# Squares of the new residual summed on TensorE, tile by tile, in the bank of the factors by token

## The chip, the cores and the metric

The kernel runs on one core of a Trainium2 chip. The metric is the device time in microseconds (us) of one execution, as the median of several runs. The engines are called TensorE (PE in the rows, with its weight loads as PEld), VectorE (DVE), ScalarE (ACT), GpSimd (POOL) and SyncE (SP, which issues most transfers). A float32 product is made of three matmuls of rounded parts: a value is split into H (rounded) and L (what is left), and H·H, L·H and H·L are summed.

## The reference

Two model blocks of two layers each run one behind the other on 512 latent tokens of width 1024; the second has 256 context tokens beside them. Each layer has a mixer and a feed-forward part. The change is in the second block, whose residual goes through a norm both behind and ahead of each part:

```
h = h + gt_m * rms_norm(y, g_post_mix[i])
f = swiglu(modulate(rms_norm(h, g_pre_ffn[i]), sh_f, sc_f), w_ffn_gate[i], w_ffn_up[i], w_ffn_down[i])
h = h + gt_f * rms_norm(f, g_post_ffn[i])
if not last:
    ... the same for the context hc
```

with `rms_norm(x, g) = x * rsqrt(mean(x * x) + eps) * g` over the 1024 features of a token, and `modulate(h, shift, scale) = h * (1 + scale) + shift`.

## The kernel before

Activations lie with features on the 128 partitions and tokens along the row: a matrix of 1024 features is KD = 8 tiles. Tokens are worked on in parts of 256: PA and PB (the latents' halves) and CT (the context). A projection takes weights unit by unit (128 output features); each unit is loaded to `raw`, split into `wH` on ScalarE and `wL` on VectorE (`hl`, L398 and L399), and multiplied by `mm3` (L416) with 24 matmuls for eight input tiles and one part.

`chain2` (L1663 and on) returns what runs between a projection out of a part and the next block's input. Its function `after(sl)` is called for one part of tokens when that part's projection is done. It is a generator: its steps are put beside the projections that follow (`defer`, `advance`), and a scheduler then orders the instructions of each engine by priority and by its own estimate of times; in a built program each engine's order is fixed. A call does this:

- It sums the squares of the projection over features: 128 columns of `acc` at a time are the stationary operand and a column of ones moves, so a 128 x 1 result has one sum per token (L527, `ss`). Square root (L529) and reciprocal (L530) make the factors by token, and `on_features` (L547, `rb`) spreads them over all partitions in a PSUM bank.
- For each of eight feature tiles it multiplies the projection by gain and factors (L1683, `ct`), and adds that to the residual (L1684, `x` or `hc`).
- Where another block follows (`nxt`), `add_square` takes the Square of the new residual on ScalarE (L518, `cs`) and adds it on VectorE to `acc` (L519). Then `rsqrt_steps` sums over features again (`ss`), makes new factors (`rb`), and `modulated` (L563 to L565) makes the next block's input, H on ScalarE and L on VectorE, which the next projection's matmuls read.

The calls with `nxt` are eight: named e2 (behind the even mixer; CT, PA, PB; next input `f2u0`), f20 (behind the first feed-forward part; CT, PA, PB; next input `ou`), and o2 (behind the odd mixer; PA, PB; next input `f2u1`). The two calls f21 at the end have no `nxt` and write the output. L1772 is the evacuation of the feed-forward part's last projections (`f`), L1753 that of its first.

Of the kernel before, what the change touches and what calls it, by code (L numbers as in the profile page):

```python
# [8 lines left out]
F32 = mybir.dt.float32  # L9
F32R = mybir.dt.float32r  # L10
BF = mybir.dt.bfloat16
AF = mybir.ActivationFunctionType
# [4 lines left out]
D = 1024  # L17
KD = 8
# [220 lines left out]
def build(tc, A, out, cst_at, vec_at, chk_at, tap=None, upto=99, mark=lambda n: None):  # L239
    nc = tc.nc  # L240
    V, S, T, G = nc.vector, nc.scalar, nc.tensor, nc.gpsimd
# [11 lines left out]
    def load(dst, src):  # L253
        nc.sync.dma_start(dst, src)
# [5 lines left out]
    def wd(sl):  # L260
        return sl.stop - sl.start
# [5 lines left out]
    state = {}  # L267
# [27 lines left out]
    def bank(tag, cols, name):  # L295
        p, rings = state["pm"]
        return p.tile([128, cols], F32, name=name, tag=tag, bufs=rings[tag], padded_shape=[128, max(cols, 512)])
# [4 lines left out]
    def ax(cols=512, name="ax"):  # L302
        return bank("ax", cols, name)
# [7 lines left out]
    def scr(tag, cols=512):  # L311

        p, w = state["sp"] if tag in ("nt", "sq") else (state["np"], {tag: 256})
        return p.tile([128, w[tag]], F32, name=tag, tag=tag, bufs=2 if tag in ("sq", "cs") else 3)[:, :cols]
# [4 lines left out]
    def C(name):  # L319
        o, n = cst_at[name]  # L320
        return cst[:, o:o + n]

    def vcol(name):
        o, n = vec_at[name]
        return vec[:, o:o + n]

    ident, ones, eps = C("ident"), C("ones"), C("eps")
# [182 lines left out]
    def add_square(acc, v, tag="sq"):  # L510

        w = v.shape[-1]
        if not acc:
            acc.append(state["np"].tile([128, 256], F32, name="acc", tag="acc", bufs=3)[:, :w])
            S.activation(acc[0], v, AF.Square)
        else:
            sq = scr(tag, w)
            S.activation(sq, v, AF.Square)  # L518
            V.tensor_tensor(acc[0], acc[0], sq, OP.add)  # L519

    def rsqrt_cols(sqs, ns, n, off, ring="ax", p=None):

        blocks = [sq[:, c:c + 128] for sq in sqs for c in range(0, sq.shape[-1], 128)]
        pc = bank(ring, 512, "ss")
        sel = ones[:, :1] if ns == 1 else C("half2")
        for b, sq in enumerate(blocks):
            T.matmul(pc[:, ns * b:ns * b + ns], sq, sel, start=True, stop=True)  # L527
        rs = (p or state["np"]).tile([128, 24], F32, name="rstd", tag="rstd", bufs=3)[:, :ns * len(blocks)]
        S.activation(rs, pc[:, :ns * len(blocks)], AF.Sqrt, bias=off, scale=1.0 / n)  # L529
        V.reciprocal(rs, rs)  # L530
        return rs

    def rsqrt_steps(sq, n, out):

        rs = rsqrt_cols([sq], 1, n, eps)
        yield
        out.extend(on_features(rs, 1, [sq.shape[-1]]))

    def on_features(rs, ns, ws, ring="ax"):

        r = 128 // ns
        c, pbs = 0, []
        for w in ws:
            pb = bank(ring, w, "rb")
            for b in range(0, w, 128):
                for i in range(ns):
                    T.matmul(pb[r * i:r * i + r, b:b + 128], rs[:, c:c + 1].to_broadcast([128, r]), ident, start=True, stop=True)  # L547
                    c += 1
            pbs.append(pb)
        return pbs  # L550

    def rsqrt_bcs(sqs, ns, n, ring="ax", p=None):
        return on_features(rsqrt_cols(sqs, ns, n, eps, ring, p), ns, [sq.shape[-1] for sq in sqs], ring)
# [4 lines left out]
    def modulated(xk, rs, a, b, h, sl, ks=range(KD)):  # L558

        for k in ks:  # L560
            t = scr("ct", wd(sl))
            hH, hL = h(0, k, sl), h(1, k, sl)
            V.scalar_tensor_tensor(t, xk(k), a[:, k:k + 1], rs, OP.mult, OP.mult)  # L563
            S.activation(hH, t, AF.Identity, bias=b[:, k:k + 1], scale=1.0)
            V.scalar_tensor_tensor(hL, t, b[:, k:k + 1], hH.bitcast(F32), OP.add, OP.subtract)  # L565
# [33 lines left out]
    def gain(name, g, sc):  # L599
        a = cp.tile([128, KD], F32, name=name)  # L600
        V.scalar_tensor_tensor(a, sc, 1.0, g, OP.add, OP.mult)
        return a

    def sub(m, i):
        return m[:, 8 * i:8 * i + 8]
# [425 lines left out]
    def chain(name, g, sc, sh):  # L1031

        box = {}
        acc = {}

        def after(sl):
            if "h" not in box:
                box["h"] = new_h(name)
                box["a"] = gain(name + "A", g, sc)
            rs = []  # L1040
            yield from rsqrt_steps(acc[sl.start][0], D, rs)
            for k in range(0, KD, 2):
                modulated(lambda k: x[:, k, sl], rs[0], box["a"], sh, box["h"], sl, range(k, k + 2))
                yield
        return box, acc, after

    mark("rglru")
    bf0, acc, after = chain("f0", vcol("nf0"), sub(mod[0], 4), sub(mod[0], 3))
# [6 lines left out]
    bm1, acc, after = chain("m1", vcol("nm1"), sub(mod[1], 1), sub(mod[1], 0))  # L1055
# [3 lines left out]
    bf1, acc, after = chain("f1", vcol("nf1"), sub(mod[1], 4), sub(mod[1], 3))  # L1059
# [5 lines left out]
    be, acc, after = chain("e", vcol("gpm0"), sub(m2[0], 1), sub(m2[0], 0))  # L1065
# [593 lines left out]
    def stream(l, sl):  # L1659
        if sl.start >= SEQ:  # L1660
            return state["hc"], slice(sl.start - SEQ, sl.stop - SEQ), mc2[l]
        return state["x"], sl, m2[l]

    def chain2(l, name, gpost, gate, nxt, yv):

        acc, gains = {}, {}

        def after(sl):
            res, rsl, m = stream(l, sl)
            c = sl.start >= SEQ  # L1670
            if c not in gains:
                a = cp.tile([128, KD], F32, name=f"{name}P{int(c)}")
                V.tensor_tensor(a, vcol(gpost), sub(m, gate), OP.mult)
                n = None
                if nxt:
                    n = gain(f"{name}A{int(c)}", vcol(nxt[1]), sub((mc2 if c else m2)[nxt[0]], nxt[2]))
                gains[c] = a, n
            a, n = gains[c]
            rs, nacc = [], []
            yield from rsqrt_steps(acc[sl.start][0], D, rs)  # L1680
            for k in range(KD):
                t = scr("ct", wd(sl))
                V.scalar_tensor_tensor(t, yv(k, sl), a[:, k:k + 1], rs[0], OP.mult, OP.mult)  # L1683
                V.tensor_tensor(res[:, k, rsl], res[:, k, rsl], t, OP.add)  # L1684
                if nxt:
                    add_square(nacc, res[:, k, rsl], "cs")
                if k % 2:
                    if not nxt:
                        load(out[:, k - 1:k + 1, sl], res[:, k - 1:k + 1, rsl])
                    yield k == KD - 1  # L1690
            if nxt:
                yield from rsqrt_steps(nacc[0], D, rs)
                h = nxt[4]()
                for k in range(0, KD, 2):
                    modulated(lambda k: res[:, k, rsl], rs[1], n, sub((mc2 if c else m2)[nxt[0]], nxt[3]), h, sl, range(k, k + 2))
                    yield
        return acc, after
# [190 lines left out]
    acc, after = chain2(0, "e2", "gom0", 2, (0, "gpf0", 4, 3, hf0), yv)  # L1888
# [6 lines left out]
    fs, cs = [], []  # L1895
    acc, after = chain2(0, "f20", "gof0", 5, (1, "gpm1", 1, 0, ho), lambda n, sl: fs[0][:, n, sl])
# [265 lines left out]
    def yv(n, sl):  # L2162
        return f[:, n, sl]

    acc, after = chain2(1, "o2", "gom1", 2, (1, "gpf1", 4, 3, hf1), yv)
# [4 lines left out]
    acc, after = chain2(1, "f21", "gof1", 5, None, yv)  # L2170
# [21 lines left out]
```

## Time and profile before

| What | Value |
|---|---|
| Time, median of 3 runs | 3222.17 us (3218.04 to 3224.64) |
| The profiled execution's own time | 3225.02 us |
| Its span, first to last instruction | 3223.3 us |
| Mean granted TensorE clock | 0.977 of full speed |
| Shares of the span in the chain of work that ended last | TensorE 61%, issue 9%, VectorE 5%, ScalarE 4% |

All times of rows are of the profiled execution, in us from the start of its span. Busy time is the time in which an engine had an instruction in work; a matmul's duration overlaps the next one's start, so the distance between starts tells what a matmul takes in a stream. The granted clock is a share of full speed (2.4 GHz; half of it is 1.2 GHz).

### The profile page before, as it was taken

The page shows a single profiled execution, that of the slowest core. Times are in us where ns is not written, and L with a number is a line of the kernel's source. Part 1 is how long each engine was busy: PE and PEld are TensorE (multiplying, and loading weights), DVE is VectorE, ACT ScalarE, POOL GpSimd, SP SyncE. Part 2 cuts the span into 40 slices and gives each one's busy share as a digit, 9 for nine tenths or more (in the row PEclk, how much of TensorE's full clock was granted, in tenths as well). Part 3 has the DMA queues.
Part 4 walks back from the last instruction along what each step waited for, and adds up shares of the span by engine and source line. Part 5 has one row for each costly group of instructions (what it writes and reads, how often), then busy time and mean ns, then how long its engine had stood idle before and what let it go on. Part 6 is the DMA issues. An engine that isn't in the chain of part 4 may idle for free.

```text
span 3223.3 us, 51513 instructions
## 1 busy us (share of the span) xinstructions
PE 3072.6 (95%) x20678; PEld 2610.6 (81%) x20678; DVE 2066.8 (64%) x4044; ACT 1472.0 (46%) x2558; POOL 17.4 (1%) x47
## 2 busy tenths in 40 slices
PE   6999999998999999998899999999997989999998
PEld 5788888975888889886667898888987867898887
DVE  7976555788787777668866684443637447572335
ACT  4965333446553335546554562212425436562222
POOL 0000000000000000000100000000000000000000
PEclk9999999997999999999899999999998999999999
DMA  7546654320256554442322433441423221242223
GB/s 233 190 151 219 196 189 163 125 66 7 73 191 202 189 196 164 135 140 90 115 70 92 136 104 118 162 146 62 158 100 131 79 91 47 75 152 94 95 99 101
DMA packets 140927, 414.72 MB, mean 129 GB/s; under 512 B 14224, under 2 KB 37520, under 8 KB 140048
## 3 DMA queue, kind: packets, MB, share of 16 engines
q1 hardware_dynamic: 138656, 400.43, 37.5%
q0 software_dynamic: 2032, 11.01, 1.1%
q8 instruction: 162, 2.65, 0.3%
q14 instruction: 77, 0.63, 0.1%
HBM read 386.74 MB, written 24.64 MB: 128 GB/s over the span
## 4 chain that ended last, share of the span: by engine, by line
PE 61%; issue 9%; DVE 5%; ACT 4%; DMA 1%; POOL 0%; DVEq 0%; ACTq 0%; POOLq 0%
PE mm L416 48%; PE po L1359 2%; PE rb L547 2%; PE ptr L1348 2%; PE S L830 1%; PE S L1402 1%; PE ss L527 1%; ACT DT L1546 1%; ACT wH L398 1%; DVE wL L399 1%; PE po L969 1%; PE sa L1575 1%; PE ptr L975 1%; DVE acc L519 0%; DVE ct L1683 0%
## 5 line engine op out<-in xcount | busy, mean ns | idle before, releaser
L398 ACT CAST wH<-raw 128x1024 fp32r<-128x1024 f32 (+4 forms) x469 | 473.0, 1012 | 1118.5 <-PE mm L416 773.6
L399 DVE TENSOR_TENSOR wL<-raw,wH 128x1024 fp32r<-128x1024 f32 (+4 forms) x469 | 549.7, 1175 | 377.8 <-ACT wH L398 370.4
L416 PE MATMUL mm<-mH,wH 128*128 128x512 f32 (+1 forms) x1104 | 377.7, 349 | 8.5 <-DVE f L1772 5.8
L416 PE MATMUL mm<-mH,wL 128*128 128x512 f32 (+1 forms) x1104 | 374.9, 347 | 1.6 <-DVE wL L399 1.6
L416 PE MATMUL mm<-mL,wH 128*128 128x512 f32 (+1 forms) x1104 | 375.3, 347 | 0.7 <-DVE mL L399 0.7
L589 DVE SCALAR_TENSOR_TENSOR raw<-raw,cond_c 128x1024 f32<-128x1024 f32 x128 | 156.4, 1224 | 154.6 <-DMA raw<-in_ada 154.4
L416 PEld LDWEIGHTS mm<-mH,wH 128*128 128x128 f32 x1104 | 206.0, 189 | 39.6 <-ACT wH L398 6.1
L416 PEld LDWEIGHTS mm<-mH,wL 128*128 128x128 f32 x1104 | 205.0, 189 | 30.5 <-DVE wL L399 2.0
L416 PEld LDWEIGHTS mm<-mL,wH 128*128 128x128 f32 x1104 | 205.5, 189 | 29.3 <-DVE mL L399 0.9
L416 PE MATMUL mm<-f2u0L,wH 128*128 128x512 f32 (+1 forms) x752 | 206.0, 327 | 0.0
L416 PE MATMUL mm<-f2u0H,wH 128*128 128x512 f32 (+1 forms) x752 | 205.7, 326 | 0.0
L416 PE MATMUL mm<-f2u0H,wL 128*128 128x512 f32 (+1 forms) x752 | 205.1, 326 | 0.0
L416 PE MATMUL mm<-f2u1H,wL 128*128 128x512 f32 (+1 forms) x432 | 151.5, 352 | 1.2 <-DVE wL L399 1.1
L416 PE MATMUL mm<-f2u1H,wH 128*128 128x512 f32 (+1 forms) x432 | 150.8, 352 | 0.6 <-ACT nt L1750 0.5
L416 PE MATMUL mm<-f2u1L,wH 128*128 128x512 f32 (+1 forms) x432 | 151.0, 351 | 0.1
L416 PEld LDWEIGHTS mm<-f2u0H,wL 128*128 128x128 f32 x752 | 125.1, 189 | 13.0
L416 PEld LDWEIGHTS mm<-f2u0H,wH 128*128 128x128 f32 x752 | 124.8, 189 | 12.6
L416 PEld LDWEIGHTS mm<-f2u0L,wH 128*128 128x128 f32 x752 | 124.8, 189 | 12.3
L626 DVE SCALAR_TENSOR_TENSOR x<-mm,mod,x 128x256 f32<-128x256 f32 (+1 forms) x112 | 66.0, 596 | 88.6 <-PE mm L416 88.5
L1753 DVE TENSOR_TENSOR nt<-nt,mm 128x512 f32<-128x512 f32 (+1 forms) x52 | 31.4, 605 | 127.3 <-PE mm L416 126.9
L416 PE MATMUL mm<-f0L,wH 128*128 128x512 f32 (+1 forms) x296 | 106.9, 361 | 0.2 <-DVE f0L L565 0.2
L416 PE MATMUL mm<-f0H,wH 128*128 128x512 f32 (+1 forms) x296 | 106.8, 361 | 0.0
(703 smaller groups left out, 7479.9 us busy)
## 6 DMA issues: line engine op xcount, KB each, us to landing
raw<-in_ada SPq DMA_DIRECT2D x192, 512.0 KB, 3.6
raw<-in_fw SPq DMA_DIRECT2D x142, 512.0 KB, 4.1
raw<-in_gw SPq DMA_DIRECT2D x125, 512.0 KB, 3.2
raw<-in_gw SPq DMA_DIRECT2D x45, 384.0 KB, 3.0
raw<-in_owin SPq DMA_DIRECT2D x25, 512.0 KB, 3.2
raw<-in_ewin SPq DMA_DIRECT2D x22, 512.0 KB, 3.3
raw<-in_awin SPq DMA_DIRECT2D x20, 512.0 KB, 3.8
raw<-in_ewout SPq DMA_DIRECT2D x18, 512.0 KB, 3.9
```

Of the source, the lines that this page charges most:

```text
L398: S.copy(H, src)
L399: V.tensor_tensor(L, src, H.bitcast(F32), OP.subtract)
L416: T.matmul(ps, W[w][:, k], h(p, k0 + k, sl), start=first and k == 0 and j == 0, stop=last and k == kt - 1 and j == 2)
L527: T.matmul(pc[:, ns * b:ns * b + ns], sq, sel, start=True, stop=True)
L547: T.matmul(pb[r * i:r * i + r, b:b + 128], rs[:, c:c + 1].to_broadcast([128, r]), ident, start=True, stop=True)
L589: V.scalar_tensor_tensor(junk, r, 1.0, c, OP.mult, OP.mult, accum_out=o[:, j:j + 1])
L626: V.scalar_tensor_tensor(x[:, n, sl], ps, gate[:, n:n + 1], x[:, n, sl], OP.mult, OP.add)
L830: T.matmul(ps, q, k[:, sl], start=j == 0, stop=j == 1)
L969: T.matmul(po[64 * half:64 * half + 64], vw[:, kt, :64], PT, start=kt == 0, stop=kt == b)
L975: T.transpose(pt[:, 128 * i:128 * i + 128], Ps[half][i][:, 128 * kt:128 * kt + 128], ident)
L1348: T.transpose(pt[:kn, c:c + 128], Ps[half][i][:, k0:k0 + kn], ident)
L1359: T.matmul(po[64 * half:64 * half + 64], vs[half], PT[:kn, half * w:half * w + w], start=j == 0, stop=j == len(keys) - 1)
```

## The change

The Square of each new residual tile no longer goes into `acc` on VectorE. It becomes the stationary operand of two matmuls (one for each 128 tokens) which sum over features and accumulate over the eight tiles in two columns of PSUM. Those columns lie in the tile `rb`, behind the 256 columns of the factors that the multiplies read. The helper `rsqrt_of` then makes the factors from these columns.

```
+    def rsqrt_of(ss, n):
+
+        rs = state["np"].tile([128, 24], F32, name="rstd", tag="rstd", bufs=3)[:, :ss.shape[-1]]
+        S.activation(rs, ss, AF.Sqrt, bias=eps, scale=1.0 / n)
+        V.reciprocal(rs, rs)
+        return rs
...
-            rs, nacc = [], []
-            yield from rsqrt_steps(acc[sl.start][0], D, rs)
+            rs = [rsqrt_cols(acc[sl.start], 1, D, eps)]
+            yield
+
+            pb = ax(512, "rb")
+            rb, ss = pb[:, :wd(sl)], pb[:, wd(sl):wd(sl) + wd(sl) // 128]
+            for b in range(0, wd(sl), 128):
+                T.matmul(rb[:, b:b + 128], rs[0][:, b // 128:b // 128 + 1].to_broadcast([128, 128]), ident, start=True, stop=True)
+            rs[0] = rb
             for k in range(KD):
                 t = scr("ct", wd(sl))
                 V.scalar_tensor_tensor(t, yv(k, sl), a[:, k:k + 1], rs[0], OP.mult, OP.mult)
                 V.tensor_tensor(res[:, k, rsl], res[:, k, rsl], t, OP.add)
                 if nxt:
-                    add_square(nacc, res[:, k, rsl], "cs")
+                    sq = scr("cs", wd(sl))
+                    S.activation(sq, res[:, k, rsl], AF.Square)
+                    for b in range(0, wd(sl), 128):
+                        T.matmul(ss[:, b // 128:b // 128 + 1], sq[:, b:b + 128], ones[:, :1], start=k == b == 0, stop=k == KD - 1 and b > 0)
...
             if nxt:
-                yield from rsqrt_steps(nacc[0], D, rs)
+                rn = rsqrt_of(ss, D)
+                yield
+                rs.extend(on_features(rn, 1, [wd(sl)]))
```

In the order of the changed program the multiply is L1696, the add L1697, the Square L1700, the pair of summing matmuls L1702 (`rb<-cst,cs 128x1 x2`, by the tile's name `rb`), the first factors L1692, the second ones L554. A note such as PE_49 names the semaphore, by its engine, that an instruction waits for.

VectorE's order at the end of f20, for PB. Before, from the first multiply by the factors on:

```order
L1683 SCALAR_TENSOR_TENSOR ct<-f_18452,f20P_23214,rb 128x256 [waits PE_49]
L1683 SCALAR_TENSOR_TENSOR ct<-f_18452,f20P_23214,rb 128x256
L399 TENSOR_TENSOR wL<-raw,wH 128x1024 [waits DMAHW5_49,Activation_49]
L1684 TENSOR_TENSOR x_17167<-x_17167,ct 128x256 [waits DVE_49] x2
L1683 SCALAR_TENSOR_TENSOR ct<-f_18452,f20P_23214,rb 128x256
L1683 SCALAR_TENSOR_TENSOR ct<-f_18452,f20P_23214,rb 128x256 [waits DVE_49]
L1684 TENSOR_TENSOR x_17167<-x_17167,ct 128x256 [waits DVE_49]
L399 TENSOR_TENSOR wL<-raw,wH 128x1024 [waits DMAHW6_49,PE_49,Activation_49]
L519 TENSOR_TENSOR acc<-acc,cs 128x256 [waits Activation_49]
L1684 TENSOR_TENSOR x_17167<-x_17167,ct 128x256 [waits DVE_49]
L519 TENSOR_TENSOR acc<-acc,cs 128x256 [waits DVE_49,Activation_49]
L1683 SCALAR_TENSOR_TENSOR ct<-f_18452,f20P_23214,rb 128x256 x2
```
After, from the same multiply on:

```order
L1696 SCALAR_TENSOR_TENSOR ct<-f_18473,f20P_23238,rb 128x256 [waits DVE_49]
L572 SCALAR_TENSOR_TENSOR ouL<-ct,m_98,ouH 128x256 [waits Activation_49] x2
L1697 TENSOR_TENSOR x_17167<-x_17167,ct 128x256 [waits DVE_49]
L1696 SCALAR_TENSOR_TENSOR ct<-f_18473,f20P_23238,rb 128x256 [waits DVE_49,PE_49]
L1697 TENSOR_TENSOR x_17167<-x_17167,ct 128x256 [waits DVE_49]
L1696 SCALAR_TENSOR_TENSOR ct<-f_18473,f20P_23238,rb 128x256 [waits PE_49]
L1697 TENSOR_TENSOR x_17167<-x_17167,ct 128x256 [waits DVE_49]
L1696 SCALAR_TENSOR_TENSOR ct<-f_18473,f20P_23238,rb 128x256 [waits PE_49]
L1697 TENSOR_TENSOR x_17167<-x_17167,ct 128x256 [waits DVE_49]
L1696 SCALAR_TENSOR_TENSOR ct<-f_18473,f20P_23238,rb 128x256 [waits PE_49]
L1697 TENSOR_TENSOR x_17167<-x_17167,ct 128x256 [waits DVE_49]
L1696 SCALAR_TENSOR_TENSOR ct<-f_18473,f20P_23238,rb 128x256 [waits PE_49]
```
The adds to `acc` are gone, and multiplies and adds alternate; each multiply but the first waits for TensorE.

TensorE's order at the same place, before, around the second sums (`ss`) and factors (`rb`) of PB, in the next block's first projection (`ou`):

```order
L416 MATMUL mm<-ouH,wL 128x256
L416 MATMUL mm<-ouH,wH 128x256
L416 MATMUL mm<-ouL,wH 128x256
L416 MATMUL mm<-ouH,wL 128x256
L527 MATMUL ss<-cst,acc 128x1 x2
L416 MATMUL mm<-ouH,wH 128x256
L416 MATMUL mm<-ouL,wH 128x256
L416 MATMUL mm<-ouH,wL 128x256
L416 MATMUL mm<-ouH,wH 128x256
L547 MATMUL rb<-cst,rstd 128x128 x2
L416 MATMUL mm<-ouL,wH 128x256
L416 MATMUL mm<-ouH,wL 128x256
```
After, from some matmuls ahead of the pairs on:

```order
L416 MATMUL mm<-ouH,wH 128x256
L416 MATMUL mm<-ouL,wH 128x256
L416 MATMUL mm<-ouH,wL 128x256
L1702 MATMUL rb<-cst,cs 128x1 x14
L416 MATMUL mm<-ouH,wH 128x256
L1702 MATMUL rb<-cst,cs 128x1 x2
L416 MATMUL mm<-ouL,wH 128x256
L416 MATMUL mm<-ouH,wL 128x256
L416 MATMUL mm<-ouH,wH 128x256
L416 MATMUL mm<-ouL,wH 128x256
```
Seven of the eight pairs stand in one row, with no matmul of the projection between them, and one matmul is ahead of the eighth.

TensorE's order at o2, PA. Before, the second factors, and the matmuls up to those that read the next block's input (`f2u1`):

```order
L547 MATMUL rb<-cst,rstd 128x128 x2
L416 MATMUL mm<-nqH,wL 128x256
L416 MATMUL mm<-gq,wH 128x256 x2
L416 MATMUL mm<-gq,wL 128x256
L416 MATMUL mm<-gq,wH 128x256 x2
L416 MATMUL mm<-gq,wL 128x256
L416 MATMUL mm<-gq,wH 128x256 x2
L416 MATMUL mm<-gq,wL 128x256
L416 MATMUL mm<-gq,wH 128x256 x2
L416 MATMUL mm<-gq,wL 128x256
L416 MATMUL mm<-f2u1H,wH 128x256 x2
L416 MATMUL mm<-f2u1L,wH 128x256
```
After, from some matmuls ahead of the last two pairs on:

```order
L416 MATMUL mm<-gq,wL 128x256
L416 MATMUL mm<-gq,wH 128x256 x2
L416 MATMUL mm<-gq,wL 128x256
L416 MATMUL mm<-gq,wH 128x256 x2
L416 MATMUL mm<-gq,wL 128x256
L416 MATMUL mm<-gq,wH 128x256 x2
L416 MATMUL mm<-gq,wL 128x256
L1702 MATMUL rb<-cst,cs 128x1 x4
L554 MATMUL rb<-cst,rstd 128x128 x2
L527 MATMUL ss<-cst,acc 128x1 x2
L416 MATMUL mm<-f2u1H,wH 128x256 x3
L416 MATMUL mm<-f2u1L,wH 128x256
```
The last two pairs, the second factors and another part's first sums stand directly ahead of the matmuls on `f2u1`; before, other matmuls of the mixer's projection (`nqH`, `gq`) stood between the factors and them.

## Rows read from the trace of the kernel before

**Rows 1.** The page: busy us of each engine (share of the span), instructions.

```profile
PE 3072.6 (95%) x20678; PEld 2610.6 (81%) x20678; DVE 2066.8 (64%) x4044; ACT 1472.0 (46%) x2558; POOL 17.4 (1%) x47
```
**Rows 2.** Busy time by stretch; columns us, PE, PEld, DVE, ACT, POOL, PEclk, DMA.

```profile
1835.00:1860.00 25.00, 24.18 (x220) 23.66 (x219) 22.24 (x46) 14.87 (x34) 0.00 (x0) 1.00 0.37 127
2480.00:2490.00 10.00, 4.82 (x41) 4.62 (x39) 9.96 (x22) 4.92 (x11) 0.00 (x0) 0.94 0.44 159
```
**Rows 3.** PE's waits: total us, times, longest; 1830-1930, 2455-2530, 2805-2865 us.

```profile
PE mm L416 <- DVE wL L399: 2.7, 2, 1.9
...
PE mm L416 <- DVE f L1772: 8.6, 2, 4.7
PE mm L416 <- DVE nkL L399: 6.1, 1, 6.1
...
PE mm L416 <- DVE wL L399: 1.1, 1, 1.1
```
**Rows 4.** Groups by line: ns minimum/median/maximum, first and last start.

```profile
L1683 DVE SCALAR_TENSOR_TENSOR ct<-y,e2P,rb x24: 471/474/479, 1843.8 to 1910.6; 128x256 f32<-128x256 f32 x24
L1683 DVE SCALAR_TENSOR_TENSOR ct<-f,f20P,rb x24: 470/473/483, 2327.3 to 2489.4; 128x256 f32<-128x256 f32 x24
L1683 DVE SCALAR_TENSOR_TENSOR ct<-f,o2P,rb x16: 472/474/480, 2813.9 to 2854.3; 128x256 f32<-128x256 f32 x16
...
L1684 DVE TENSOR_TENSOR x<-x,ct x64: 411/417/422, 1874.3 to 3219.4; 128x256 f32<-128x256 f32 x64
...
L519 DVE TENSOR_TENSOR acc<-acc,cs x63: 409/417/427, 1253.1 to 2858.3; 128x256 f32<-128x256 f32 x63
...
L518 ACT ACTIVATE cs<-x x42: 399/416/465, 1875.2 to 2856.5; 128x256 f32<-128x256 f32 x42
...
L527 PE MATMUL ss<-cst,acc x132: 164/250/353, 223.4 to 3211.8; 128*128 128x1 f32 x132
```
**Rows 5.** PE's timeline at e2: start us, us, instruction (one pair is x4).

```profile
1857.02 0.40 PE L416 MATMUL mm<-o,wH 128*128 128x256 f32 x2
1857.25 0.55 PE L527 MATMUL ss<-cst,acc 128*128 128x1 f32 x4
1857.66 0.36 PE L416 MATMUL mm<-o,wL 128*128 128x256 f32 x1
1857.86 0.40 PE L416 MATMUL mm<-o,wH 128*128 128x256 f32 x2
```
**Rows 6.** The page's costliest groups: busy us, mean ns, idle before.

```profile
L398 ACT CAST wH<-raw 128x1024 fp32r<-128x1024 f32 (+4 forms) x469 | 473.0, 1012 | 1118.5 <-PE mm L416 773.6
L399 DVE TENSOR_TENSOR wL<-raw,wH 128x1024 fp32r<-128x1024 f32 (+4 forms) x469 | 549.7, 1175 | 377.8 <-ACT wH L398 370.4
```
**Rows 7.** PE's timeline at the end of f20, PA and PB.

```profile
2445.20 0.68 PE L547 MATMUL rb<-cst,rstd 128*128 128x128 f32 x4
...
2478.46 0.60 PE L547 MATMUL rb<-cst,rstd 128*128 128x128 f32 x4
...
2490.94 0.58 PE L416 MATMUL mm<-ouH,wH 128*128 128x256 f32 x1 [6.12 <-DVE nkL L399]
...
2491.75 0.93 PE L527 MATMUL ss<-cst,acc 128*128 128x1 f32 x4
2492.54 0.56 PE L416 MATMUL mm<-ouH,wH 128*128 128x256 f32 x1
...
2493.54 1.05 PE L547 MATMUL rb<-cst,rstd 128*128 128x128 f32 x4
```
**Rows 8.** The timeline at the end of the program (f21), all engines.

```profile
3210.89 0.42 DVE L519 TENSOR_TENSOR acc<-acc,sq 128x256 f32<-128x256 f32 x1 [0.54 <-ACT sq L518]
...
3211.46 0.58 PE L527 MATMUL ss<-cst,acc 128*128 128x1 f32 x4 [1.58 <-DVE acc L519]
3212.07 0.26 ACT L529 ACTIVATE rstd<-ss,cst 128x2 f32<-128x2 f32 x1 [1.22 <-PE ss L527]
3212.37 0.17 DVE L530 RECIPROCAL rstd<-rstd 128x2 f32<-128x2 f32 x1 [1.06 <-ACT rstd L529]
```
## The prediction

> **What bounds the kernel now.** I read the page first. TensorE is busy 95% of the span, VectorE 64%, ScalarE less [rows 1], so I ask of every edit what it adds to TensorE's stream and what it makes TensorE wait for. The other views are of the stretches in which the changed function runs with squares: e2 (CT, PA, PB) from 1844 us on, f20 from 2327 (CT) to 2494 (PB's end), o2 from 2814 [rows 4, 7]. Busy time by stretch shows two kinds of place [rows 2]. At e2, CT to PB, TensorE has 24.18 of 25 us and VectorE 22.24: TensorE is the bound, VectorE has little room. At the end of f20 TensorE has 4.82 of 10 us and VectorE 9.96: there VectorE is the bound. TensorE's waits agree [rows 3]: at e2 2.7 us in all, at the end of f20 14.7, at o2 1.1 for weights; everywhere the waited-for engine is VectorE.
>
> **The change, part by part.** What goes: the sum of squares was seven adds a call on VectorE and one pair of one-column matmuls at its end. Of the 63 adds [rows 4] seven stand in an earlier function, so 56 go, in eight calls. They cost VectorE 0.42 us each, some 0.34 us where several follow each other: 56 × 0.34 = 19 us of VectorE. That is worth time only where TensorE waits for VectorE.
>
> What comes: eight pairs a call in place of one, so 56 pairs more on TensorE. The nearest row is the old pair itself, the same shapes. It starts at 1857.25, the next matmul at 1857.66 (0.41 us), the one after 0.20 later instead of 0.12 [rows 5]: **0.47 to 0.49 us a pair** with what it delays. 56 × 0.47 = 26.3 us. At six of the eight sites TensorE is busy or paced by the rounds below: 42 × 0.47 = **+19.7**. Nothing hides it there. At f20 PA and PB it is part of a sum of its own.
>
> What changes shape: the sums now stand in the bank of the factors, which VectorE reads. In the changed order every multiply but the first of a call carries a wait for TensorE, that is for the pair of the tile before. So a call becomes a ring: pair (TensorE), multiply, add (VectorE), Square (ScalarE), pair. Before, VectorE ran two multiplies and two adds ahead and the summing trailed. The engine times are 0.41 + 0.47 + 0.42 + 0.42 = 1.72 [rows 4, 5]; a hand-over between engines takes 0.03 (pair to root), 0.04 (root to reciprocal) or 0.15 us (add to pair) [rows 8], four of them about 0.3. **One round is 2.02 us** if nothing stands between.
>
> Here a rule speaks against the change. The Trainium skill, "PSUM — Partial Sum Buffer", section "PSUM bank collisions raise a hardware error", says that two engines must not touch the same bank and quadrant at once, not even at different columns, and that semaphores should guard by bank. That explains the wait on a tile that VectorE doesn't read; with guards by address alone, the sum would be the 26.3 us of pairs less some relief. No row of before shows it, since none has two such users in a bank; the changed order does.
>
> In front of each pair TensorE has n matmuls of 256 columns at 0.12 us (two start in 0.23, [rows 5]). With n × 0.12 + 0.47 ≥ 2.02, n ≥ 13, the ring hides. Counted in the changed order: e2 CT 22, 20, 19, 13, 13, 13, 13; e2 PB 24, 13, 19, 18, 13, 17, 21; o2 PB 22, 24, 24, 24, 24, 20, 13; f20 CT 7 to 14 matmuls of 512 columns, at 0.23 us. These just hide it, so I give the four of them 1.2 + 0.7 + 0.3 + 0.5 = 2.7 us for rounds a little longer. But e2 PA has 20, 20, 24, 24, 24, **0, 0**, and o2 PA 14, 20, 24, 24, 24, 12, **0**. Each zero exposes 2.02 − 0.47 = 1.55. Behind the last pair stand root (0.26), reciprocal (0.17) and hand-overs, 0.62 in all, then the first multiply and the first ScalarE cast of the next block's input, about 1.0; before, 13 (o2) to 22 (e2) other matmuls covered this, now none does: 1.6. So e2 PA is 2 × 1.55 + 0.5 (the input's other tiles come at VectorE's pace) + 1.6 = 5.2, o2 PA 1.55 + 0.5 + 0.3 + 1.6 = 3.9. Together with the 2.7: **+11.8**. After such holes the clock falls: behind a wait of 6.12 us matmuls stand 0.21 apart and a pair holds TensorE 0.79 us [rows 7]. For two smaller holes I take 1.5 each: **+3** (0 to 6). Of the 3.8 us of waits for weights at e2 and o2 [rows 3] half may go, since VectorE has less to do: **−2** (0 to −4).
>
> f20 PA and PB: from PA's first factors to PB's second ones it was 2493.54 − 2445.20 = 48.3 us, 33.3 for PA and 15.1 for PB [rows 7]. PA afterwards: 184 matmuls × 0.12 = 22.1, eight pairs 3.8, other sums and factors 0.9, and 1.7 left of waits, 28.5; the 8.6 us of waits for the evacuation (f, L1772) mostly go, because VectorE now alternates between the ring and the evacuations. That is −5. PB: its first multiply is now queued behind PA's next-block input: two casts of 1.18 [rows 6] and eleven multiplies of some 0.40, 6.7 us; the first pair comes at 9.0. Then all pairs but the last stand on TensorE in one row with no matmul between. Nothing covers seven rounds, at the lower clock (pair 0.9, round 2.5): 17.5. With the last pair, root, factors and some slow matmuls about 29 against 15.1: +14. The next projection's matmuls, their evacuation (nkL) and weight casts are queued behind. Net **+9** (5 to 13).
>
> The sum: 19.7 + 11.8 + 3 − 2 + 9 = 41.5, rounded to **+41**. The profiled execution took 3225.0 us (span 3223.3), so 3266 by it. It lay 2.9 us above the median of the three runs, so I say **3263**.
>
> **The rivals.** (A) The forecast, chance 0.50, own range +30 to +55, that is 3252 to 3277.
> (B) The ring hides everywhere, or the program has the time for it elsewhere: only the pairs are paid, and relief and f20 cancel. +20 to +28, 3242 to 3250. For it: the six sites mostly have n ≥ 13. Against: the zeros in the order, and f20 PB. Chance 0.20.
> (C) Rounds are longer: a weight cast on ScalarE (1.01 us) or VectorE (1.18) [rows 6] falls into the ring in half of the rounds. At e2 and o2 20 rounds exceed their cover by 0.8: 16 us; at f20 PB seven by 1.05: 7. 41 + 23 = +64, 3286. For it: VectorE's 22.24 of 25 us [rows 2] means that casts must stand somewhere between. Against: the order can place them while the ring waits. Chance 0.17.
> (D) The other side: VectorE's relief is what counts. If the ring hides, the freed 19 us remove TensorE's waits at e2, f20 and o2 (2.7 + 14.7 + 1.1 = 18.5) and behind them some 5 us (an estimate: 60 matmuls at 0.21 instead of 0.12, [rows 7]), while f20's pairs fall into its idle time. 19.7 − 23.5 = −4; it decides from f20 PB's rounds being covered and a pair under 0.40 us, and at 0.33 it gives −10, 3212. For it: 14.7 us of waits at f20 really are for VectorE. Against: the pair's price is read in TensorE's stream, and the seven uncovered rounds are in the order. Chance of faster 0.06.
> (E) The same with half of these gains: 19.7 − 18.5 = +1, no change that can be measured. Chance 0.07.
>
> **How the numbers follow.** About 0.2% (6.4 us) is what a measurement of this kernel can tell from no change. Slower is A, B and C: 0.87; same 0.07; faster 0.06. The time is A's, 3263. The range takes in B's lower part and C's middle, with the bounds of the unknown costs (f20 5 to 13, clock 0 to 6, relief 0 to −4): 3236 to 3294; outside remain D, E and the long end of C, some 0.2.
>
> **What would show it.** In the profile after: 64 pairs under the new line at some 0.25 us a pass, TensorE's busy time up by about 20 us; multiplies on VectorE waiting for TensorE, spaced by 2.0 us or more within a call; at e2 PA and o2 PA new waits of TensorE for Square, around 1.5 us each, and for the next block's input; at f20 PB a stretch of some 17 us in which TensorE does pairs alone, at a lower granted clock, and the waits for f L1772 much shorter. Wrong it would be if pairs cost under 0.3 us in the stream, if the multiplies don't wait, or if PA's evacuation waits stay as they were (then +46 or more).

## The result

| | Median, us | Lowest to highest | Runs |
|---|---|---|---|
| Before | 3220.1 | 3217.4 to 3224.6 | 4 |
| After | 3266.7 | 3264.8 to 3274.3 | 4 |

The change makes the kernel slower: ratio 1.0149, 95% interval 1.0137 to 1.0161, some 48 us of 3220 (44 to 52). The forecast was 3263 with a range of 3236 to 3294. The profiled execution took 3274.3 us (span 3272.2), 7.6 above the median.

The page of the changed kernel, busy times and the shares of the chain, which answer to [rows 1]:

```profile
span 3272.2 us, 51884 instructions
PE 3112.3 (95%) x20902; PEld 2642.9 (81%) x20902; DVE 2055.5 (63%) x3988; ACT 1466.0 (45%) x2554; POOL 17.4 (1%) x47
...
PE 64%; issue 8%; ACT 4%; DVE 4%; DMA 0%; POOL 0%; ACTq 0%; DVEq 0%; POOLq 0%
```
The span is 48.9 us longer, TensorE's busy time 39.7, and VectorE's 11.3 shorter. TensorE's share stays 95%, so the page alone doesn't show the new waits. Busy time also counts pairs and matmuls that the lower clock stretches, which is one reason why it grew by more than the 20 us that the forecast named.

The multiplies by the factors grouped by line (VectorE; ns minimum, median, maximum; first and last start), and below them what VectorE sat idle for ahead of them (us, times):

```profile
L1696 DVE SCALAR_TENSOR_TENSOR ct<-y,e2P,rb x24: 471/480/483, 1847.2 to 1935.3; 128x256 f32<-128x256 f32 x24
L1696 DVE SCALAR_TENSOR_TENSOR ct<-f,f20P,rb x24: 475/480/481, 2349.0 to 2523.6; 128x256 f32<-128x256 f32 x24
L1696 DVE SCALAR_TENSOR_TENSOR ct<-f,o2P,rb x16: 473/476/481, 2848.0 to 2910.2; 128x256 f32<-128x256 f32 x16
L1696 DVE SCALAR_TENSOR_TENSOR ct<-f,f21P,rb x16: 470/473/481, 3242.6 to 3267.6; 128x256 f32<-128x256 f32 x16
...
  PE rb L1702: 32.3, 27
```
Against [rows 4] a multiply takes as long as before, but VectorE waits 32.3 us in 27 places for the pairs. The first starts also divide the span into stages. The row for f21 of the kernel before, which [rows 4] leave out:

```profile
L1683 DVE SCALAR_TENSOR_TENSOR ct<-f,f21P,rb x16: 471/472/480, 3193.1 to 3218.7; 128x256 f32<-128x256 f32 x16
```
From e2 to f20 it was 483.5 us and is 501.8 (+18.3), from f20 to o2 486.6 and 499.0 (+12.4), from o2 to f21 379.2 and 394.6 (+15.4). The 3.4 us ahead of e2's first multiply are not the change's: nothing is edited there, and over this study's profiled executions that multiply came anywhere from 1834.7 to 1847.2. Stages have a spread too: where two kernels do the same calls in the same way, a stage differed by 0.1 to 3.2 us between their executions.

TensorE's waits in three stretches (e2, the end of f20, o2), as in [rows 3]:

```profile
PE rb L1702 <- ACT cs L1700: 3.9, 3, 1.6
PE rb L554 <- DVE rstd L537: 0.9, 1, 0.9
PE mm L416 <- ACT f2u0H L571: 0.7, 1, 0.7
...
PE rb L1702 <- ACT cs L1700: 15.8, 7, 6.5
PE mm L416 <- DVE nkL L399: 1.4, 1, 1.4
...
PE rb L1702 <- ACT cs L1700: 3.2, 2, 1.9
PE mm L416 <- ACT f2u1H L571: 1.9, 2, 1.1
...
PE rb L554 <- DVE rstd L537: 1.4, 2, 0.8
```
The waits for `wL` and for f (L1772) are gone; the forecast had half of the first and most of the second going. In their place TensorE waits for Squares, and at e2 and o2 for second factors and for the next block's input. The Squares at the end of f20 cost 15.8 us in seven places.

Busy time by stretch, columns as in [rows 2]; the last column but two is the granted clock:

```profile
1845.00:1870.00 25.00, 24.98 (x201) 23.86 (x201) 16.27 (x32) 12.54 (x30) 0.00 (x0) 1.00 0.41 142
1895.00:1920.00 25.00, 19.52 (x128) 18.84 (x128) 14.31 (x33) 11.43 (x23) 0.00 (x0) 0.80 0.11 39
2508.00:2518.00 10.00, 3.77 (x16) 3.43 (x16) 3.62 (x8) 1.66 (x4) 0.00 (x0) 0.50 0.00 0
```
At e2 CT TensorE is still full, and VectorE, at 22.24 of 25 in the nearest stretch of [rows 2], has fallen to 16.27: it waits. What the ring costs there is not idle time of TensorE but longer pairs, as shown below. Around e2 PA's end TensorE has 19.52 of 25, and the clock is 0.80. In the middle of f20 PB TensorE has 3.77 of 10 us, VectorE 3.62 and ScalarE 1.66: no engine is busy half of the time, each waits for the next one, and the granted clock is 0.50, its lower level of 1.2 GHz.

One round of the ring at e2 PA, engines together (start, duration, engine, instruction, idle before and whom for):

```profile
1898.17 0.61 PE L1702 MATMUL rb<-cst,cs 128*128 128x1 f32 x4 [0.78 <-ACT cs L1700]
1898.82 0.48 DVE L1696 SCALAR_TENSOR_TENSOR ct<-y,e2P,rb 128x256 f32<-128x256 f32 x1 [1.61 <-PE rb L1702]
1899.33 0.42 DVE L1697 TENSOR_TENSOR x<-x,ct 128x256 f32<-128x256 f32 x1
1899.85 0.42 ACT L1700 ACTIVATE cs<-x 128x256 f32<-128x256 f32 x1 [1.73 <-DVE x L1697]
1900.32 0.61 PE L1702 MATMUL rb<-cst,cs 128*128 128x1 f32 x4 [1.54 <-ACT cs L1700]
...
1902.49 1.01 PE L1702 MATMUL rb<-cst,cs 128*128 128x1 f32 x4 [1.56 <-ACT cs L1700]
...
1904.35 1.19 PE L554 MATMUL rb<-cst,rstd 128*128 128x128 f32 x4 [0.85 <-DVE rstd L537]
...
1906.93 1.01 PE L416 MATMUL mm<-f2u0H,wH 128*128 128x256 f32 x3 [0.75 <-ACT f2u0H L571]
```
Pair, multiply, add, Square, pair: from 1898.17 to 1900.32 is 2.15 us, with 2.17 to the next. The forecast said 2.02. The multiply starts 0.65 us behind the start of the pair, whose four passes take 0.61; the forecast had put in 0.41 for the pair, the distance to the next matmul's start. The hand-overs (0.04, 0.03, 0.10 and 0.05) are shorter than its 0.3. Behind the last pair stand the second factors at 1904.35 and the first matmul on the next input at 1906.93, with only PB's first sums (`ss`) between them.

TensorE's timeline at f20 PB, to be held against [rows 7]:

```profile
2498.38 0.61 PE L1692 MATMUL rb<-cst,rstd 128*128 128x128 f32 x4
...
2507.13 1.02 PE L1702 MATMUL rb<-cst,cs 128*128 128x1 f32 x4 [6.46 <-ACT cs L1700]
2509.68 1.01 PE L1702 MATMUL rb<-cst,cs 128*128 128x1 f32 x4 [1.54 <-ACT cs L1700]
2512.26 1.02 PE L1702 MATMUL rb<-cst,cs 128*128 128x1 f32 x4 [1.56 <-ACT cs L1700]
...
2522.57 1.01 PE L1702 MATMUL rb<-cst,cs 128*128 128x1 f32 x4 [1.56 <-ACT cs L1700]
...
2524.95 0.58 PE L416 MATMUL mm<-ouH,wH 128*128 128x256 f32 x1 [1.37 <-DVE nkL L399]
...
2528.32 1.05 PE L554 MATMUL rb<-cst,rstd 128*128 128x128 f32 x4
```
From PB's first factors to its second ones it is now 29.9 us, against 15.1; forecast 29. The rounds are 2.55 to 2.58 us long (forecast 2.5), and the first pair comes 8.75 us behind the factors (forecast 9.0).

### The profile page after: what moved, and what is told of

Read it like the earlier page. It is cut to its first block, busy times and chain, and to the rows that moved or that the text cites. A ratio compares the mean times of both kernels' runs of the same rounds, so it can differ in the third digit from the quotient of the medians.

```text
span 3272.2 us, 51884 instructions
## 1 busy us (share of the span) xinstructions
PE 3112.3 (95%) x20902; PEld 2642.9 (81%) x20902; DVE 2055.5 (63%) x3988; ACT 1466.0 (45%) x2554; POOL 17.4 (1%) x47
## 4 chain that ended last, share of the span: by engine, by line
PE 64%; issue 8%; ACT 4%; DVE 4%; DMA 0%; POOL 0%; ACTq 0%; DVEq 0%; POOLq 0%
PE mm L416 50%; PE po L1366 2%; PE ptr L1355 2%; PE rb L554 1%; PE S L837 1%; PE rb L1702 1%; PE S L1409 1%; PE ss L527 1%; ACT DT L1553 1%; PE po L976 1%; ACT wH L398 1%; PE sa L1582 1%; PE ptr L982 1%; ACT P L1342 0%; PE st L1627 0%
## 5 line engine op out<-in xcount | busy, mean ns | idle before, releaser
L399 DVE TENSOR_TENSOR wL<-raw,wH 128x1024 fp32r<-128x1024 f32 (+4 forms) x469 | 549.9, 1175 | 370.7 <-ACT wH L398 363.4
L416 PEld LDWEIGHTS mm<-f2u0L,wH 128*128 128x128 f32 x752 | 126.2, 191 | 13.1
```

Of the source, the lines that this page charges most:

```text
L399: V.tensor_tensor(L, src, H.bitcast(F32), OP.subtract)
L416: T.matmul(ps, W[w][:, k], h(p, k0 + k, sl), start=first and k == 0 and j == 0, stop=last and k == kt - 1 and j == 2)
```

## The experiments

All were timed beside the kernel before on the same chip. A ratio is to the kernel before, with its 95% interval; the us behind it are its share of 3220.

**A bank of its own for the sums.**

```
-            rb, ss = pb[:, :wd(sl)], pb[:, wd(sl):wd(sl) + wd(sl) // 128]
+            rb = pb[:, :wd(sl)]
+            ss = ax(512, "ssq")[:, :wd(sl) // 128] if nxt else None
```

> The pairs stay, but their two columns stand in a bank of their own; in the built order no multiply but the first of a call waits for TensorE any more. My theory (pairs cost 0.47 us each in TensorE's stream, and the ring through the shared bank costs about as much again): 56 x 0.47 = 26 us of pairs remain, less up to 10 us for VectorE's relief and for pairs that fall into TensorE's idle time at f20, so +16 to +26 against before, about 3236 to 3246; TensorE's waits for the Square fall from 23 us to under 5. Rival 1 (the pairs themselves cost it all, 46.6 / 56 = 0.83 us each): it stays at about 3265. Rival 2 (VectorE's relief is what counts once the ring is gone): 3220 or less.

Measured: 3238.8 us, ratio 1.0054 (1.0039 to 1.0069), +17 us. Both rivals fall: with the same 64 pairs in the program, nearly two thirds of the loss are gone once the pairs and the factors don't share a bank: 31 us, 24 to 37 by the two intervals. No multiply sat idle for a pair in this kernel, and TensorE's waits for Squares in the three stretches fell from 22.9 us to 3.6, at e2 and at the end of f20:

```profile
PE ssq L1703 <- ACT cs L1701: 0.2, 1, 0.2
...
PE ssq L1703 <- ACT cs L1701: 3.4, 3, 1.5
```
A pair in this kernel, at e2 (PEld is the weight load, here of the Square's columns):

```profile
1853.84 0.40 PE L416 MATMUL mm<-o,wH 128*128 128x256 f32 x2
1853.96 0.53 PEld L1703 LDWEIGHTS ssq<-cst,cs 128*128 128x128 f32 x4
...
1854.08 0.50 PE L1703 MATMUL ssq<-cst,cs 128*128 128x1 f32 x4
...
1854.44 0.36 PE L416 MATMUL mm<-o,wL 128*128 128x256 f32 x1
...
1854.64 0.28 PE L416 MATMUL mm<-o,wH 128*128 128x256 f32 x1
```
The first load starts at 1853.96, under matmuls in flight, and the pair takes TensorE from 1854.08 on; four starts (two matmuls, the pair, one matmul) use 0.80 us, of which three matmuls are 0.36: 0.44 a pair. The changed kernel at the same place of e2 CT:

```profile
1858.79 0.42 ACT L1700 ACTIVATE cs<-hc 128x256 f32<-128x256 f32 x1
...
1859.26 0.52 PEld L1702 LDWEIGHTS rb<-cst,cs 128*128 128x128 f32 x4 [0.19 <-ACT cs L1700]
1859.26 0.61 PE L1702 MATMUL rb<-cst,cs 128*128 128x1 f32 x4
...
1859.73 0.48 PE L416 MATMUL mm<-o,wH 128*128 128x256 f32 x2
```
Here the Square ends at 1859.21 and the load can start only at 1859.26; the next matmul starts 0.47 behind the pair, and the pair itself stood 0.15 later than the stream would have let it. Worked out in this way over the pairs that have matmuls ahead of them and no wait in their own row, a pair takes 0.62 us on average at e2 and o2 in the changed kernel (30 pairs), 0.48 at e2 with a bank of its own (20 pairs). The Trainium skill, "PSUM — Partial Sum Buffer", section "Engine vs sequencer instructions", says that TensorE's queue lets a weight load overlap matmuls in flight; these rows agree for the kernel with a bank of its own, and in the ring the load starts only when the last matmul is nearly done, since its operand is made just in time.

**Pairs beside the adds, into a bank that nobody reads.** To the kernel before:

```
+            more = ax(512, "ssq")[:, :wd(sl) // 128] if nxt else None
...
-                    add_square(nacc, res[:, k, rsl], "cs")
+                    sq = add_square(nacc, res[:, k, rsl], "cs")
+                    for b in range(0, wd(sl), 128):
+                        T.matmul(more[:, b // 128:b // 128 + 1], sq[:, b:b + 128], ones[:, :1], start=k == b == 0, stop=k == KD - 1 and b > 0)
```

`add_square` here also returns the tile that holds the Square.

> The kernel before, with the adds on VectorE and the old sums kept, plus the same pairs of one-column matmuls on each of the eight squares of a call, into a bank of their own that nobody reads: the price of 64 pairs without ring and without relief. My theory: 64 x 0.47 = 30 us, of which the 16 pairs at f20 PA and PB may lie in idle time: +22 to +31, 3242 to 3251. Rival 1 (a pair costs 0.8 us): +50, 3270. Rival 2 (a pair costs only what its four passes take beyond their overlap, some 0.1 us each way): under +15, 3235 or less.

Measured: 3246.8 us, ratio 1.0076 (1.0051 to 1.0102), +24.5 us for 64 pairs, 0.38 a pair (0.26 to 0.51). Both rivals fall, the second one narrowly (+16 is the lower end of the interval, and it had said under +15). By its three stages the profiled execution was 12.0, 8.8 and 6.8 us longer than before's, 27.6 in all, 0.43 a pair.

**The same pairs, in the bank of the factors.** The edit above, with `more` behind the factors as in the change:

```
-            yield from rsqrt_steps(acc[sl.start][0], D, rs)
...
+            pb = ax(512, "rb")
+            rb, more = pb[:, :wd(sl)], pb[:, wd(sl):wd(sl) + wd(sl) // 128]
...
```

> As the run with pairs beside the kept adds, but the pairs' columns, which nobody reads, stand in the bank of the factors: adds, pairs and ring together, without VectorE's relief. My theory (the ring through the shared bank costs about 29 us by itself, the difference between the changed kernel and the one with a bank of its own): 3247 + 29 and some more, since an add on VectorE now stands in the ring: 3272 to 3285. Rival (the 29 us are not the ring, but come from the squares' sum being ready late): within 8 us of the run with pairs beside, 3255 or less.

Measured: 3275.9 us, ratio 1.0174 (1.0157 to 1.0191), +56 us: 31 more than in a bank of their own (22 to 41). Here nobody needs the sums, so they can't be late; only the shared bank is different, and with it the order that the scheduler makes. This is the plainest evidence for the ring. Between the changed kernel and the one with its own bank it was 48 − 17 = 31 as well. The tile `rb` and the bank are the same 512 columns here, so the runs don't tell a wait that goes by tile from one that goes by bank.

**VectorE's relief alone.** To the kernel before:

```
-                    add_square(nacc, res[:, k, rsl], "cs")
+                    if nacc:
+                        S.activation(scr("cs", wd(sl)), res[:, k, rsl], AF.Square)
+                    else:
+                        add_square(nacc, res[:, k, rsl], "cs")
```

> The kernel before without the seven adds of squares in a call (the second sums of a call cover its first feature tile alone; the Squares are still taken, the pair at the end stays): VectorE's relief by itself, 56 x 0.34 = 19 us of VectorE. My theory: TensorE is the bound nearly everywhere, so only f20 PA and PB and some waits for weights give anything: -2 to -9, 3211 to 3218. Rival 1 (relief removes all of the 18.5 us of waits for VectorE): -18 or more, under 3203. Rival 2 (nothing): within 2 us of before.

Measured: 3207.7 us, ratio 0.9960 (0.9947 to 0.9973), −13 us (−17 to −9). That is more than my theory gave and less than the rival's 18. By stages: e2 −1.7, f20 −5.6, o2 −3.4, together −10.7.

**f20 as before.** To the changed kernel:

```
-            rb, ss = pb[:, :wd(sl)], pb[:, wd(sl):wd(sl) + wd(sl) // 128]
+            rb, ss, nacc = pb[:, :wd(sl)], pb[:, wd(sl):wd(sl) + wd(sl) // 128], []
+            pairs = name != "f20"
...
-                if nxt:
+                if nxt and not pairs:
+                    add_square(nacc, res[:, k, rsl], "cs")
+                elif nxt:
...
-                rn = rsqrt_of(ss, D)
+                rn = rsqrt_of(ss, D) if pairs else rsqrt_cols([nacc[0]], 1, D, eps)
```

> The changed kernel with the three calls of f20 done as before (adds on VectorE, one pair at the end); e2 and o2 as in the change. My theory (every call pays for itself, by the distances between the same points of the two traces f20 costs 3.8 at CT and 8.5 to 9.3 at PA and PB): 12 to 13 us less than the changed kernel, 3253 to 3255. Rival (the seven uncovered rounds at f20 PB lie beside waits that would be there anyway): less than 6 us less, 3261 or more.

Measured: 3251.8 us, ratio 1.0100 (1.0076 to 1.0124), +32 us: 16 less than the changed kernel. The rival falls; my 12 to 13 lies within the noise of that difference. The stage from f20 to o2 was 484.4 us in it, 14.6 less than the changed kernel's 499.0, and 2.2 less than in the kernel before, which does f20 in the same way.

**PA of e2 and o2 as before.** The same edit with another condition:

```
+            pairs = not (name in ("e2", "o2") and sl.start == 0)
```

> The changed kernel with e2 PA and o2 PA done as before (the two calls whose last pairs have no matmul ahead of them in TensorE's order); CT and PB of e2, all of f20, and o2 PB as in the change. My theory: seven pairs (3.3 us), the holes (5.2 and 3.9) and the slower clock behind them (1.5) go at each: 16 to 20 us less than the changed kernel, 3247 to 3251. Rival (the holes are a matter of the order and turn up at the next call instead): under 10 us less, above 3257.

Measured: 3237.9 us, ratio 1.0071 (1.0052 to 1.0090), +23 us: 25 less than the changed kernel, where I had said 16 to 20. The stage e2 to f20 is 488.7 us, 13.1 less than in the changed kernel, and o2 to f21 385.9, 8.7 less, together 21.8. Another 3.2 lie at f20, where both kernels do the same, and may be the executions' own spread. The rival's price falls. At e2 TensorE has no wait for a Square left. At o2 the rival's mechanism does show: the last pair of PB now has three matmuls ahead of it, and TensorE waits there for its Square,

```profile
PE rb L1705 <- ACT cs L1703: 1.4, 1, 1.4
```
which it did not do at PB in the changed kernel. The two calls with pairs that have no matmul ahead of them bear nearly half of the loss, their own pairs included.

**Two tiles at a time, in the shared bank.** In the changed kernel the pairs of tiles k − 1 and k are issued behind every odd k:

```
-                    for b in range(0, wd(sl), 128):
-                        T.matmul(ss[:, b // 128:b // 128 + 1], sq[:, b:b + 128], ones[:, :1], start=k == b == 0, stop=k == KD - 1 and b > 0)
+                    two = [sqs, sq] if k % 2 else []
+                    sqs = sq
+                    for i, v in enumerate(two):
+                        for b in range(0, wd(sl), 128):
+                            T.matmul(ss[:, b // 128:b // 128 + 1], v[:, b:b + 128], ones[:, :1], start=k == 1 and i == b == 0, stop=k == KD - 1 and i == 1 and b > 0)
```

> The changed kernel, same shared bank and the same 64 pairs, but the pairs of two tiles are issued together behind every second tile: VectorE waits for TensorE once in two tiles. My theory: a round of two tiles takes two multiplies, two adds, one Square and two pairs, some 3.2 us in place of 4.0, and the matmuls ahead of it cover nearly all of that at e2 and o2; most of the ring's 29 us goes: 3240 to 3250. Rival (what counts is that a pair and a reader are in one bank, however rarely they wait): above 3258.

Measured: 3236.8 us, ratio 1.0051 (1.0034 to 1.0068), +16 us, as good as a bank of its own and 3 us below the 3240 of my theory. What VectorE sat idle for ahead of the multiplies in this kernel:

```profile
  PE rb L1705: 17.1, 22
```
It still waits 22 times for pairs, but 17.1 us in all, and one of two multiplies runs ahead of the wait. TensorE has no wait for a Square left at e2 and o2. The rival falls: sharing a bank does not cost by itself; a hand-over in every tile does, with the order that the scheduler builds around it.

**Pairs at f20 PA and PB alone, in a bank of their own.** The edits of the own bank and of the condition together, to the changed kernel; with them e2, o2 and f20 CT are as in the kernel before (`c` is true for CT):

```
+            rb, nacc = pb[:, :wd(sl)], []
+            pairs = name == "f20" and not c
+            ss = ax(512, "ssq")[:, :wd(sl) // 128] if nxt and pairs else None
...
```

> The kernel before, with pairs in a bank of their own at f20 PA and PB alone, where TensorE waits for VectorE: 14 adds less on VectorE, 14 more pairs that may fall into TensorE's idle time. By the run with a bank of its own everywhere (that stage was 5.9 us longer, of which CT's seven pairs are about 3): -2 to +4, 3217 to 3223. Rival (the pairs are free there and the relief of 5.6 us in this stage, seen without the adds, stays): -4 to -6, 3213 to 3215.

Measured: 3223.0 us, ratio 1.0013 (1.0003 to 1.0023), +4 us (1 to 7), at the upper end of my theory; the rival falls. At the end of f20 TensorE waits for f (L1772 of before) once, 3.9 us, instead of twice, 8.6, and not for `nkL`, but 3.4 us for Squares. So 7.4 us less of waits stand against 14 more pairs, some 5 us at 0.38, and yet the stage from f20 to o2 is 488.2 us against 486.6. Where the rest went is not shown.

**The adds on GpSimd.** To the kernel before, for the squares of these calls:

```
-    def add_square(acc, v, tag="sq"):
+    def add_square(acc, v, tag="sq", E=None):
...
-            V.tensor_tensor(acc[0], acc[0], sq, OP.add)
+            (E or V).tensor_tensor(acc[0], acc[0], sq, OP.add)
...
-                    add_square(nacc, res[:, k, rsl], "cs")
+                    add_square(nacc, res[:, k, rsl], "cs", G)
```

> The kernel before with the adds of a call's squares on GpSimd instead of VectorE, nothing on TensorE: VectorE's relief, which was worth 11 to 13 us when the adds were left out, without the pairs' price. My theory: -4 to -12, 3207 to 3215, if seven GpSimd adds keep pace with the tiles. Rival (an add takes GpSimd above 1.3 us, or slows VectorE beside it, so the second sums come late): at or above 3222.

Measured: 3245.2 us, ratio 1.0074 (1.0058 to 1.0090), +24 us; the rival held. The adds on GpSimd (ns minimum, median, maximum), and a wait of TensorE at e2:

```profile
L519 POOL TENSOR_TENSOR acc<-acc,cs x56: 722/788/3959, 1849.6 to 2879.8; 128x256 f32<-128x256 f32 x56
```
```profile
PE ss L527 <- POOL acc L519: 11.4, 3, 5.3
```
The median add takes 0.79 us, but the longest 3.96, and all 56 take 63.5 us; the second sums wait for the last of them, 21.6 us over e2, f20 and o2. The trace shows where the long ones lie. The twelve adds with VectorE idle beside them took 0.72 to 0.73 us. All eleven above 1.4 us ran beside a weight split on VectorE (L399) for 0.8 us or more; the longest, at 1885.60, beside two, 2.4 us of them, and 1.4 us of VectorE's other work. VectorE's own adds stayed at 0.42.

**Half of the adds on GpSimd.** To the kernel before (the first tile's Square makes `nacc`; `nacc2` is a second `acc`):

```
+                    if k < 4:
+                        ...
+                            G.tensor_tensor(nacc[0], nacc[0], sq, OP.add)
+                    else:
+                        add_square(nacc2, res[:, k, rsl], "cs")
...
-                yield from rsqrt_steps(nacc[0], D, rs)
+                V.tensor_tensor(nacc2[0], nacc2[0], nacc[0], OP.add)
+                yield from rsqrt_steps(nacc2[0], D, rs)
```

> The kernel before, with the squares of a call's first four tiles summed on GpSimd and of the last four on VectorE, and one more add on VectorE to join them: four adds a call on VectorE in place of seven, nothing more on TensorE. My theory: GpSimd's three adds (1.1 us each on average in the run with all seven there) end before VectorE's last ones, so the chain's end is no later, and three sevenths of the 11 to 13 us of relief come: -3 to -6, 3214 to 3217. Rival (GpSimd beside VectorE takes several us for an add, so the joining add waits): 3222 or more.

Measured: 3217.4 us, ratio 1.0000 (0.9991 to 1.0009). Neither the gain of the theory nor the rival's loss: a gain above 3 us is excluded. By its stages the profiled execution was 4.6 us shorter, of which the timed runs show nothing, so this stays inconclusive. No version that keeps the sums whole beats the kernel before.

## Why the prediction was right, point by point

**What bounds the kernel.** Right. TensorE's work and waits made the time, and VectorE's relief moved little: 13 us when nothing takes its place, 4 to 5 us where pairs come in (pairs beside against own bank: 24.5 − 17 = 7 us, of which eight more pairs are 3; in the shared bank 56 − 48 = 8).

**The parts of the sum.** Of the 48 us, 56 pairs at 0.38 are 21 and the ring 31; the −4 that is left over goes to the relief. The sum was grouped by places, and there it says:

| Place | Forecast, us | Measured by stage, us |
|---|---|---|
| e2: pairs 9.9, rounds and holes 7.1, clock 1.5, relief −1.4 | 17.1 | 18.3 |
| f20: CT 3.8, PA and PB 9 | 12.8 | 12.4 |
| o2: pairs 6.6, rounds and holes 4.2, clock 1.5, relief −0.5 | 11.8 | 15.4 |

At f20 both halves were right: PA 27.7 us from its first factors (2470.69) to PB's (forecast 28.5), PB 29.9 (29). At e2 PA the five waits in the rows above sum to 5.5 us, where 5.2 was forecast. That e2 as a whole fits within 1.2 us is in part luck: by the run with PA as before, PA cost 13.1 (forecast 10.0), so CT and PB together cost 5.2 (forecast 7.1).

**What was mis-sized.** First, "One round is 2.02 us". The bare ring takes 2.15, because VectorE waits for all of the pair's 0.61 and not for its 0.41. So 13 matmuls ahead don't quite hide it: the four rounds of e2 CT with 13 ahead are 2.15 us long, the ring's own time.

Second, the term "42 × 0.47". In the 37 covered rounds of e2, o2 and f20 CT a pair takes 0.61 beyond the matmuls, since its Square comes just when TensorE gets there. That is 0.14 × 37 = 5 us, of which the 2.7 us for rounds a little longer stood for half. Rounds with 19 to 24 matmuls ahead, which the bare ring would fit into, pay it too: ScalarE often has something else ahead of the Square. In 22 of the 64 tiles that is a weight cast, at o2 in 11 of 16. At e2 PA, where the add was done at 1893.74:

```profile
1893.83 1.05 ACT L398 CAST wH<-raw 128x1024 fp32r<-128x1024 f32 x1 [1.55 <-PE mm L416]
1894.78 0.41 ACT L1700 ACTIVATE cs<-x 128x256 f32<-128x256 f32 x1
```
Elsewhere it is the evacuation of a projection's tile (at 1858.24 and 1858.51, ahead of the Square at 1858.79 shown above). So rival C's mechanism came true, at some 0.15 us a round and not 0.8, since the matmuls ahead cover most of it. Where few do, it shows: the two pairs with 12 matmuls ahead waited 0.78 us (e2 PA, 1898.17, an evacuation ahead of the Square) and 1.34 (o2 PA, 2869.38, a weight cast). The forecast had counted 24 matmuls ahead of the first of them.

Third, o2. I gave PB 0.3 us, but TensorE waited there 0.80 for the second factors (at 2913.62) and 1.11 for the next input (2915.42). The first of these has a cause that the forecast left out: ScalarE loads a table for the square root.

```profile
2911.72 1.28 ACT L536 ACT_TABLE_LOAD   x1
2911.75 0.61 PE L1702 MATMUL rb<-cst,cs 128*128 128x1 f32 x4
2913.01 0.26 ACT L536 ACTIVATE rstd<-rb,cst 128x2 f32<-128x2 f32 x1
```
The pair ends at 2912.36, but the root starts at 2913.01, when the load is done. At PA it was 4.5 us in four waits, where 3.4 was forecast for rounds, root and first input. How o2's excess of 3.6 us divides between PA and PB is open: the run with PA as before gives 8.7 us for PA, as forecast, but in it PB has a new wait for a Square.

**The shared bank.** The multiplies waited, as the changed order said. The Trainium skill, "PSUM — Partial Sum Buffer", section "PSUM bank collisions raise a hardware error", asks for such guards by bank and quadrant; the waits agree with it, and what the runs add is the price of a wait per tile, 31 us, and that two tiles at a time leave nearly none of it. That a read without the guard would go wrong was not tried.

**The rivals.** B is nearly what the kernel with its own bank shows, +17 us where B had +20 to +28: in the shared bank the ring did not hide. C's casts stood in the ring, but cost a small part of its 23 us. D and E needed the relief to remove 18 us of waits; left out altogether, the adds gave 13, and the pairs cost more than that.

## What to carry to other kernels

Before moving a small sum to the engine that is the bound, read the price of the same shape in that engine's stream, and multiply. Look at which bank an accumulation stands in and who reads that bank: a result that one engine reads tile by tile and another adds to tile by tile makes one chain out of two engines that ran beside each other; a bank of its own, or several tiles for each hand-over, takes it apart. And look in the built order for the places where the chain's last steps have nothing ahead of them: two such calls of eight bore nearly half of the loss here. Ask there, too, whether a table load stands ahead of the root.

## What was not expected of the hardware

- The first multiply of e2, with no edit ahead of it, came between 1834.7 and 1847.2 us in the profiled executions; a comparison of two spans carries this, one of stages only the stages' own spread, up to 3.2 us here.
- An add of 128 x 256 on GpSimd took from 0.72 to 3.96 us in one run, VectorE's about 0.42 throughout. The long ones stood beside VectorE's weight splits; that this makes them long was not tried by a run of its own.
- A table load of 1.28 us ahead of a square root on ScalarE held the root back by 0.65 us behind its sums, where nothing covered it (o2 PB).
